# Gates of the merge made ahead of the pooling, top-k rounds tile by tile: a reordering of filler work in a fused three-branch decoder layer

## The chip, the cores and the metric

The kernel runs on one core of one Trainium2 chip. A core has five engines that run their own queues in order: TensorE (PE, matmuls, with its weight loads shown as PEld), VectorE (DVE), ScalarE (ACT), GpSimd (POOL) and SyncE (SP), which issues DMA transfers; POOL issues some as well. The time is the device time of one execution in microseconds, and the median of several executions counts. Less is better.

## The reference

One decoder layer on x of 512 x 1024 float32. One input projection makes all that three branches need; each branch is gated, projected, weighted by a per-channel sigmoid and added; an output projection, a scaled residual and a LayerNorm end it.

```
u = x @ w_in + b_in                       # split into 19 pieces
y_a = pool_mixer(a_x) * silu(a_z)         # A: trailing means over windows 2, 4, 8, 16 (4 groups of 128 channels),
                                          #    minus x, then a 128x128 matmul per group
y_b = dsa(b_q, b_k, b_v, i_q, i_k, i_w) * silu(b_z)
                                          # B: an indexer scores all keys, each query keeps its 128 best causal
                                          #    keys, 8 heads attend to these with one shared key and value
y_c = nsa(c_q, ..., c_g) * silu(c_z)      # C: 8 heads in 2 groups: compressed blocks, selected blocks, window;
                                          #    three softmaxes, gated per head
g = sigmoid(g_merge)                      # 512 x 3 x 1024
m = g[:,0] * (y_a @ w_pa) + g[:,1] * (y_b @ w_pb) + g[:,2] * (y_c @ w_pc)
out = layernorm(2**0.25 * x + m @ w_o)
```

Top-k is min(256, 512 // 4) = 128 keys, so the first tile of 128 queries needs no selection: top-k concerns the query tiles j = 1, 2 and 3, whose score rows are 256, 384 and 512 long.

## The kernel before

Everything large is kept transposed, channels on partitions, the 512 positions along the free axis. float32 matmuls are made from two-part splits: a high part and a remainder, three matmuls for one product (`mm3`, lines 68 to 70). x is split once into xh and xl. The weights come in tiles of 128 output channels x 1024 inputs; `load_w` (line 87) loads one into a staging tile, ACT copies the high part (line 93), POOL subtracts for the remainder (line 95; DVE does it at the start and end of the kernel). There are 2 staging tiles and 3 each of high and low parts, so the next tiles are made while one is used.

`dense(i)` (line 142) is one such tile: 8 steps, each of three 128x128 by 512 matmuls into one PSUM bank (pool `pd`, 3 banks), with a `yield` after each step. On it stand: `queries` (ACT and DVE split the result), `silu2` (two ACT passes into two tiles, one DVE pass), `gate_d` (line 597: one ACT tanh of a merge gate into a tile `tg` of tag "b"), `pool_x` (line 556), `pool_z` (line 577), `keypair`. `pool_x(g)` copies the result to SBUF on ACT, makes the trailing sums by g + 1 shifted adds with small copies on POOL (lines 566, 567), the mean minus x by four DVE instructions (lines 570 to 573) and splits it into `ph` (ACT line 64, DVE line 65). `pool_y(g)` (line 582) is one step: three matmuls of `ph` with the group's matrix, then DVE at line 588 multiplies with the gate `za` of `pool_z(g)`, and a split.

`merge(br, d)` (line 621) is one of 8 channel tiles of one branch's projection: before its own 4 steps (`branch_d`: a weight tile of 128 x 512, tile `pp` in PSUM, one DVE pass at line 614) it runs `merge_g(br, d + 1)`, the 8 steps of the next tile's gate, so a merge has 12 steps. For branches 2 and 1, POOL adds the product to the sum (line 632).

Attention is made in units (`Unit`, line 410): kind "c" for branch C, two groups g, query tiles j = 3, 2, 1, 0, two parts br (selected blocks together with the compressed ones, and window); then kind "b" for branch B, g = 0 and 1, j = 0 to 3. A unit has one or two sub-units. `front(u)` makes scores on PE into a PSUM bank (pool `pq`, 4 banks; line 441), adds the mask and takes the maximum on DVE (line 443), exponentiates on ACT (line 448), normalises into high and low float16 parts `pc` or `pb` (ACT line 460, DVE line 462) and transposes them by a DMA on SP's queue. `back` is the product with the values on PE (line 479), two sub-units later (`LAG = 2`), with `finish` (line 534) behind it.

**Order.** PE's order is the program's own (`manual_schedule`), the other engines' is made by a planner that simulates the program; `tc.high_priority()` lifts the weight splits and evacuations there. The dense work between the attention is a list of generators, the stream `F` (line 731). The loop over units gives it credit: `F.step(3.25)` after each half of a front, `F.step(2)` after a sub-unit, 0.3 per step of a back; in the index stage 2 per score. One credit is one `yield`. A string in the list, "c0" or "c1", is a mark: as long as the flag of that name is not set, the stream stops there and its credit is dropped (line 694). The flag c0 (c1) is set when the last unit of group 0 (1) of branch C is finished. `F.until` runs the stream on to a named item where a unit needs it.

Top-k takes 16 rounds per tile, each of one MAX8 and one MATCH_REPLACE8 (with the load of its values) over the score row `acc{j}` in place; `topk_end` turns the marked row into the mask of unit b{g}{j}. The list `rounds` (line 742) goes through j = 1, 2, 3 in turn. `tk(2.3)` after each sub-unit, ordered behind its last DVE instruction, takes 2.3 rounds on average; whatever is left goes at the first unit b of j > 0 (`tk(100)`).

Of the kernel before, what the change touches and what calls it, by code (L numbers as in the profile page):

```python
# [7 lines left out]
F32 = mybir.dt.float32  # L8
# [11 lines left out]
KT = D // 128  # L20
# [14 lines left out]
def trunk(ctx, tc, a, out, dbg=None):  # L35
# [12 lines left out]
    def big(tag, name, dt=F32, shape=(128, 2, 512)):  # L48
        return bp.tile(list(shape), dt, tag=tag, name=name, bufs=BUFS[tag])
# [13 lines left out]
    def split(h, l, src):  # L63
        nc.scalar.activation(h, src, AF.Copy)
        nc.vector.tensor_sub(l, src, f(h))  # L65
# [76 lines left out]
    def dense(i, s0=0, ps=None):  # L142
        wh, wl = early[i][1:] if i in early else load_w(a["wt"][i], 1024, f"w{i}")
        ps = (ps or dps)(f"d{i}")
        n = S - s0
        for k in range(KT):
            w = slice(k * 128, k * 128 + 128)
            mm3(ps[:, :n], wh[:, w], wl[:, w], X(0, k, s0), X(1, k, s0), k == 0, k == KT - 1)
            yield
        return ps[:, :n], bias[:, i:i + 1]  # L150
# [388 lines left out]
    def psum_acc():  # L539

        turn[0] ^= 1
        return ACC[:, turn[0]]
# [51 lines left out]

    M32 = []

    def gate_d(d, br):
        i = I_G + 3 * d + br
        ps, b = yield from dense(i)
        t = big("b", "tg", F32, (128, 512))  # L600
        with tc.high_priority():
            nc.scalar.activation(t, ps, AF.Tanh, scale=0.5, bias=bhalf[:, i:i + 1])
        return t

    def branch_d(d, br, Y, t, dst):
        wh, wl = load_w(a["wp"][br, d], 512, f"wp{br}")
        ps = dps("pp")
        for e in range(4):
            w = slice(e * 128, e * 128 + 128)
            yh, yl = Y[e // 2]  # L610
            mm3(ps, wh[:, w], wl[:, w], yh[:, e % 2], yl[:, e % 2], e == 0, e == 3)
            yield
        with tc.high_priority():
            nc.vector.scalar_tensor_tensor(dst, t, 1.0, ps, op0=OP.add, op1=OP.mult)  # L614

    tg, YS, MH, ML = {}, {}, [], []

    def merge_g(br, d):
        tg[br, d] = yield from gate_d(d, br)

    def merge(br, d):
        if d + 1 < KT:
            yield from merge_g(br, d + 1)
        t = tg[br, d]
        if br == 0:
            if d % 2 == 0:
                M32.append(big("t", f"m{d}"))
            yield from branch_d(d, 0, YA, t, M32[d // 2][:, d % 2])
        else:
            yield from branch_d(d, br, YS[br], t, t)  # L630
            m = M32[d // 2][:, d % 2]
            nc.gpsimd.tensor_add(m, m, t)  # L632
            if br == 1:
                if d == 0:
                    MH.extend(big("pt", f"mh{i}", F32R, (128, 4, 512)) for i in range(2))
                    ML.extend(big(t, f"ml{i}", F32R) for i, t in enumerate("sspp"))
                split(MH[d // 4][:, d % 4], ML[d // 2][:, d % 2], m)
                dbg(f"m{d}", m)
# [84 lines left out]
    for n in (2, 1, 1, 1, 1, 1, 2):  # L723
        for _ in range(n):
            st.step()
        for _ in range(n):
# [2 lines left out]
    mcmp, rowv = small["mcmp"].rearrange("p (j n) -> p j n", j=NT), small["rowv"]  # L729
    POOL[0] = True  # L730
    F = Stream([(compress_in, I_KC, "k"), (vscales,), (compress_in, I_VC, "v"), (f_zc, 0, 0), (compress_mid, "k"),
                (f_zc, 0, 1), (compress_k,), (compress_mid, "v"), (f_qc, 1, 0), (f_qc, 1, 1), (f_pool,), (compress_v,),
                (pool_x, 0), (pool_x, 1), (pool_z, 0), (pool_z, 1), (f_kk, 1), (pool_y, 0), (f_zc, 1, 0), (pool_y, 1),
                (pool_x, 2), (pool_x, 3), (f_zc, 1, 1), (pool_z, 3), (pool_z, 2), (pool_y, 2), (f_qb, 0, 0), (pool_y, 3),
                (merge_g, 0, 0), "c0", (f_qb, 0, 1)] + [(merge, 0, d) for d in range(4)] +
               [(f_zb, 0, 0), (f_zb, 0, 1)] + [(merge, 0, d) for d in range(4, 7)] +
               [(merge_g, 2, 0), (merge, 0, 7), "c1", (f_qb, 1, 0), (f_qb, 1, 1), (f_zb, 1, 0), (f_zb, 1, 1)] +
               [(merge, 2, d) for d in range(KT)])
    ix = Stream([(index_scores, j) for j in (1, 2, 3)])
    while ix.step():  # L740
        F.step(2)
    rounds = [(topk_round, j) for _ in range(16) for j in (1, 2, 3)] + [(topk_end, j) for j in (1, 2, 3)]
    tkn = [0.0]

    def tk(n):
        tkn[0] += n
        while rounds and tkn[0] >= 1:
            tkn[0] -= 1
            fn, j = rounds.pop(0)
            fn(j)  # L750

    work = []
    for g in range(2):
# [11 lines left out]
    def flush(limit):  # L765

        while backs and backs[0][0] <= limit:
            _, un, w = backs.pop(0)
            if limit == 1000:
                F.step(8)  # L770
            kind, g, j, br = w
            if kind == "c":
                F.until(("vscales",), ("compress_v",), ("f_zc", g, 0), ("f_zc", g, 1))
            for _ in un.back(br == 0):
                F.step(0.3)
            if kind == "b":
                F.until(("f_zb", g, 0), ("f_zb", g, 1))
                finish(un.acc, j, zb[g], YB[g])
            elif br == 1:
                cmps[g, j].back(un.acc)  # L780
                finish(un.acc, j, zc[g], YC[g])
                if j == 0:
                    flags.add(f"c{g}")
                    if g == 1:
                        split_y(2, YC)

    for w in work:
        kind, g, j, br = w
        if kind == "c":
            if br == 0:  # L790
                accs[w[:3]] = psum_acc()
            F.until(("compress_k",), *([("f_kk", g)] if g else []), *([("f_qc", g, e) for e in range(2)] if g else []))
            if j == 3 and br == 0:
                YC.append(big("t", f"yc{g}"))
            gv = GS[:, j, :].rearrange("p (h b) -> p h b", b=3)
            if br == 0:
                cmps[g, j] = Compressed(g)
            un = Unit(f"c{g}{j}{br}", accs[w[:3]], j, qc[g], kk[g][br], cmask[:, (3 - j) * 128:],
                      1 + 2 * br + g, gv[:, 4 * g:4 * g + 4, 1 + br], None if br else cmps[g, j])
        else:  # L800
            F.until(("f_qb", g, 0), ("f_qb", g, 1))
            if j == 0:
                YB.append(big("t", f"yb{g}"))
            if j:
                tk(100)
            un = Unit(f"b{g}{j}", psum_acc(), j, qb[g], KB[0], cmask[:, 384:] if j == 0 else negm[j],
                      0, None)
        for u in range(un.nsub):
            for _ in un.front(u):
                F.step(3.25)  # L810
            with tc.issue_after(un.last.ins):
                tk(2.3)
            nsub += 1
            F.step(2)
            flush(nsub - LAG)
        backs.append((nsub, un, w))
# [165 lines left out]
```

## Time and profile before

| | |
|---|---|
| median of 3 runs | 550.96 us (550.22 to 551.14) |
| profiled execution | 547.52 us, span 545.7 us |
| PE busy, mean granted clock | 519.2 us (95%), 0.976 |
| DVE, ACT, POOL busy | 381.6 (70%), 278.7 (51%), 217.8 us (40%) |
| dense matmuls (tile d) of weight tiles, lines 68 to 70 | 3 x 424, 0.39 us each |
| weight splits on POOL, 128x1024 / 128x512 | 41 x 2.44 us / 16 x 1.28 us |

The profile is of one execution. A row of a list in order of time begins with the start and the duration in us; a line in square brackets is the wait in front and what ended it. A matmul's duration overlaps the next one's: the distance of two starts is what it costs. "x8" counts instructions. Rows by group give busy us and the mean in ns.

### The profile page before, as it was taken

What the parts mean: (1) busy time and instruction counts of PE and PEld (TensorE: products, weight loads), DVE (VectorE), ACT (ScalarE), POOL (GpSimd) and SP (SyncE); (2) the same over time, 40 slices, a digit from 0 to 9 for tenths busy, and PEclk for the clock granted to TensorE, in tenths of its full rate; (3) what the DMA queues carried; (4) which work ended last, traced back from release to release, by engine and by line L of the source; (5) the groups of instructions that cost most, each with busy time, mean ns of one, the idle gap of its engine ahead of it and who ended that gap; (6) DMA issues with size and microseconds to landing.
All of it is one profiled execution on the core that took longest, in us unless ns stands there. A gap on an engine that the chain in (4) does not pass through costs nothing.

```text
span 545.7 us, 7778 instructions
## 1 busy us (share of the span) xinstructions
PE 519.2 (95%) x2718; PEld 420.2 (77%) x2718; DVE 381.6 (70%) x928; ACT 278.7 (51%) x561; POOL 217.8 (40%) x190
## 2 busy tenths in 40 slices
PE   7999989989999876999999999999999999999993
PEld 4899878868778654877778877787878888887883
DVE  5774898999999999888766466666441544545366
ACT  6783466655565475546566585765632333442000
POOL 0325433465557441134544355355564211316043
PEclk8999999989999997899999999999999999999997
DMA  7622331436545243365544445545553336454012
GB/s 271 261 77 78 115 117 59 121 79 154 95 114 126 64 116 82 84 165 129 154 102 114 123 130 132 126 117 127 139 140 96 117 111 207 164 185 144 1 60 94
DMA packets 82135, 66.72 MB, mean 122 GB/s; under 512 B 67184, under 2 KB 68656, under 8 KB 82096
## 3 DMA queue, kind: packets, MB, share of 16 engines
q1 hardware_dynamic: 74912, 40.54, 27.8%
q0 software_dynamic: 7184, 25.69, 15.4%
q8 instruction: 21, 0.34, 0.3%
q14 instruction: 18, 0.15, 0.1%
HBM read 47.87 MB, written 2.10 MB: 92 GB/s over the span
## 4 chain that ended last, share of the span: by engine, by line
PE 56%; DVE 9%; DMA 2%; ACT 1%; issue 1%; DVEq 0%; ACTq 0%
PE d L68 10%; PE d L70 10%; PE d L69 10%; PE pp L68 4%; PE pp L70 4%; PE pp L69 4%; PE acc L479 3%; PE wo L70 2%; PE wo L68 2%; PE wo L69 2%; PE qkb L441 2%; PE qkc L441 2%; DMA wo_st<-in_wo_dram 1%; DVE acc L306 1%; DVE m L305 1%
## 5 line engine op out<-in xcount | busy, mean ns | idle before, releaser
L68 PE MATMUL d<-xh,w_h 128*128 128x512 f32 (+1 forms) x424 | 168.6, 398 | 5.6 <-DVE za L588 2.8
L70 PE MATMUL d<-xh,w_l 128*128 128x512 f32 (+1 forms) x424 | 166.2, 392 | 0.0
L69 PE MATMUL d<-xl,w_h 128*128 128x512 f32 (+1 forms) x424 | 166.0, 392 | 0.0
L95 POOL TENSOR_TENSOR w_l<-w_st,w_h 128x1024 fp32r<-128x1024 f32 x41 | 99.8, 2436 | 130.1 <-ACT w_h L93 129.2
L68 PEld LDWEIGHTS d<-xh,w_h 128*128 128x128 f32 x424 | 80.5, 190 | 23.7 <-DVE za L588 3.3
L70 PEld LDWEIGHTS d<-xh,w_l 128*128 128x128 f32 x424 | 80.4, 190 | 17.5 <-DVE w_l L95 0.4
L69 PEld LDWEIGHTS d<-xl,w_h 128*128 128x128 f32 x424 | 80.5, 190 | 14.0
L93 ACT ACTIVATE w_h<-w_st 128x1024 fp32r<-128x1024 f32 x53 | 56.1, 1059 | 52.0 <-DMA w_st<-in_wt_dram 23.4
L448 ACT ACTIVATE qkc<-qkc,nb 128x512 f32<-128x512 f32 (+3 forms) x64 | 32.1, 502 | 44.3 <-DVE nb L443 28.6
L632 POOL TENSOR_TENSOR m<-m,tg 128x512 f32<-128x512 f32 x16 | 21.7, 1355 | 56.2 <-DVE tg L614 54.5
L95 POOL TENSOR_TENSOR wp_l<-wp_st,wp_h 128x512 fp32r<-128x512 f32 x16 | 20.5, 1281 | 53.9 <-ACT wp_h L93 53.9
L462 DVE SCALAR_TENSOR_TENSOR pc<-qkc,r,pc 128x512 f16<-128x512 f32 (+3 forms) x64 | 32.6, 543 | 8.6 <-ACT pc L460 8.3
L460 ACT ACTIVATE pc<-qkc,r 128x512 f16<-128x512 f32 (+3 forms) x64 | 29.6, 525 | 12.7 <-issue 5.5
L443 DVE CUSTOM_DVE_ANT_0 qkc<-qkc,cmask 128x512 f32<-128x512 f32 (+3 forms) x64 | 31.3, 490 | 4.4 <-PE qkc L441 4.0
L95 DVE TENSOR_TENSOR w_l<-w_st,w_h 128x1024 fp32r<-128x1024 f32 x12 | 15.6, 1306 | 19.4 <-ACT w_h L93 19.4
L448 ACT ACTIVATE qkb<-qkb,nb 128x128 f32<-128x128 f32 (+3 forms) x32 | 16.0, 500 | 23.3 <-DVE nb L443 23.0
L92 POOL DMA_DIRECT2D w_st<-in_wt_dram x41 | 23.3, 568 | 10.2 <-POOL w_l L95 6.8
L70 PE MATMUL wo<-woh,ml 128*128 128x512 f32 (+1 forms) x72 | 26.4, 367 | 0.3 <-DVE ml L65 0.3
L69 PE MATMUL wo<-wol,mh 128*128 128x512 f32 (+1 forms) x72 | 26.3, 366 | 0.0
L68 PE MATMUL wo<-woh,mh 128*128 128x512 f32 (+1 forms) x72 | 26.3, 365 | 0.0
L306 DVE MATCH_REPLACE8 acc<-m,acc 128x256 f32<-128x256 f32 (+2 forms) x48 | 25.7, 540 | 0.0
L479 PEld LDWEIGHTS <-vh 128*64 128x64 f16 x240 | 13.8, 110 | 15.1 <-issue 15.1
(245 smaller groups left out, 1031.7 us busy)
## 6 DMA issues: line engine op xcount, KB each, us to landing
w_st<-in_wt_dram POOLq DMA_DIRECT2D x41, 512.0 KB, 3.7
w_st<-in_wt_dram SPq DMA_DIRECT2D x12, 512.0 KB, 4.6
wp_st<-in_wp_dram POOLq DMA_DIRECT2D x16, 256.0 KB, 3.0
wo_st<-in_wo_dram SPq DMA_DIRECT2D x8, 512.0 KB, 3.5
xst<-in_xT_dram SPq DMA_DIRECT2D x8, 256.0 KB, 5.1
wp_st<-in_wp_dram SPq DMA_DIRECT2D x8, 256.0 KB, 2.6
z<-in_x_dram SPq DMA_DIRECT2D x4, 512.0 KB, 4.9
wvst<-in_wve_dram SPq DMA_DIRECT2D x4, 320.0 KB, 6.9
```

Of the source, the lines that this page charges most:

```text
L68: nc.tensor.matmul(ps, wh, rh, start=start, stop=False)
L69: nc.tensor.matmul(ps, wh, rl, start=False, stop=False)
L70: nc.tensor.matmul(ps, wl, rh, start=False, stop=stop)
L92: (nc.gpsimd if POOL[0] else nc.sync).dma_start(st, src)
L93: nc.scalar.activation(h[:, :n], st, AF.Copy)
L95: eng.tensor_sub(l[:, :n], st, f(h[:, :n]))
L306: nc.vector.match_replace(negm[j], m8, negm[j], MARK)
L443: nc.vector.tensor_tensor_reduce(sc[i], sc[i], self.mask, -0.125, 3e38, OP.add, OP.min, nb[:, i:i + 1])
L448: nc.scalar.activation(sc[i], sc[i], AF.Exp, scale=-1.0, bias=nb[:, i:i + 1], accum_out=den[:, i:i + 1])
L460: nc.scalar.activation(p[:, 0, i], sc[i], AF.Copy, scale=r[:, i:i + 1])
L462: self.last = nc.vector.scalar_tensor_tensor(p[:, 1, i], sc[i], r[:, i:i + 1], p[:, 0, i], op0=OP.mult, op1=OP.subtract)
L479: nc.tensor.matmul(self.acc[64 * i:64 * i + 64], v[:, k, self.vs * 64:self.vs * 64 + 64], pw[:, z, i, k], start=first, stop=False, skip_gr ...
```

## The change

The order of the filler stream and the rate of the top-k rounds are changed; no instruction is added or dropped.

- A new item `early_g(br, d)` makes the gate of channel tile d into one half of a tile of tag "s" (two tiles hold four gates). The four gates d = 0 to 3 of branch 0 stand between the compression and the pooling's items, those of branch 2 just in front of the mark "c1". `merge` skips the gate of the next tile where it is there already: merge(0, 0 to 2) and merge(2, 0 to 2) have 4 steps instead of 12.
- The pooling's items come later and in another order: pool_z and pool_y follow their pool_x more closely, and `f_pool` (the load and split of the pooling matrices) later as well. f_kk(1) and f_zc(1, 0) come ahead of them, f_qb(0, 0) goes behind "c0".
- Top-k: all rounds of j = 1 and 2 in turn with their ends, then those of j = 3. After each sub-unit 1.7 rounds instead of 2.3, and at unit b{g}{j} only what is left of tile j (`tk_until`).

```diff
--- before.py
+++ after.py
@@ -594,10 +594,10 @@
 
     M32 = []
 
-    def gate_d(d, br):
+    def gate_d(d, br, t=None):
         i = I_G + 3 * d + br
         ps, b = yield from dense(i)
-        t = big("b", "tg", F32, (128, 512))
+        t = big("b", "tg", F32, (128, 512)) if t is None else t
         with tc.high_priority():
             nc.scalar.activation(t, ps, AF.Tanh, scale=0.5, bias=bhalf[:, i:i + 1])
         return t
@@ -618,8 +618,16 @@
     def merge_g(br, d):
         tg[br, d] = yield from gate_d(d, br)
 
+    EG = {}
+
+    def early_g(br, d):
+
+        if d % 2 == 0:
+            EG[br] = big("s", f"eg{br}{d}", F32)
+        tg[br, d] = yield from gate_d(d, br, EG[br][:, d % 2])
+
     def merge(br, d):
-        if d + 1 < KT:
+        if d + 1 < KT and (br, d + 1) not in tg:
             yield from merge_g(br, d + 1)
         t = tg[br, d]
         if br == 0:
@@ -729,17 +737,19 @@
     mcmp, rowv = small["mcmp"].rearrange("p (j n) -> p j n", j=NT), small["rowv"]
     POOL[0] = True
     F = Stream([(compress_in, I_KC, "k"), (vscales,), (compress_in, I_VC, "v"), (f_zc, 0, 0), (compress_mid, "k"),
-                (f_zc, 0, 1), (compress_k,), (compress_mid, "v"), (f_qc, 1, 0), (f_qc, 1, 1), (f_pool,), (compress_v,),
-                (pool_x, 0), (pool_x, 1), (pool_z, 0), (pool_z, 1), (f_kk, 1), (pool_y, 0), (f_zc, 1, 0), (pool_y, 1),
-                (pool_x, 2), (pool_x, 3), (f_zc, 1, 1), (pool_z, 3), (pool_z, 2), (pool_y, 2), (f_qb, 0, 0), (pool_y, 3),
-                (merge_g, 0, 0), "c0", (f_qb, 0, 1)] + [(merge, 0, d) for d in range(4)] +
-               [(f_zb, 0, 0), (f_zb, 0, 1)] + [(merge, 0, d) for d in range(4, 7)] +
-               [(merge_g, 2, 0), (merge, 0, 7), "c1", (f_qb, 1, 0), (f_qb, 1, 1), (f_zb, 1, 0), (f_zb, 1, 1)] +
-               [(merge, 2, d) for d in range(KT)])
+                (f_zc, 0, 1), (compress_k,), (compress_mid, "v"), (f_qc, 1, 0), (f_qc, 1, 1), (compress_v,),
+                (early_g, 0, 0), (f_kk, 1), (early_g, 0, 1), (f_pool,), (f_zc, 1, 0), (pool_x, 0), (early_g, 0, 2),
+                (pool_z, 0), (pool_x, 1), (early_g, 0, 3), (pool_y, 0), (pool_z, 1), (f_zc, 1, 1), (pool_x, 2), (pool_y, 1),
+                (pool_z, 2), (pool_x, 3), (pool_y, 2), (pool_z, 3), (pool_y, 3),
+                "c0", (f_qb, 0, 0), (f_qb, 0, 1)] + [(merge, 0, d) for d in range(3)] + [(f_zb, 0, 0), (f_zb, 0, 1)] +
+               [(merge, 0, d) for d in range(3, 7)] + [(early_g, 2, 0), (merge, 0, 7)] +
+               [(early_g, 2, d) for d in range(1, 4)] +
+               ["c1", (f_qb, 1, 0), (f_qb, 1, 1), (f_zb, 1, 0), (f_zb, 1, 1)] + [(merge, 2, d) for d in range(KT)])
     ix = Stream([(index_scores, j) for j in (1, 2, 3)])
     while ix.step():
         F.step(2)
-    rounds = [(topk_round, j) for _ in range(16) for j in (1, 2, 3)] + [(topk_end, j) for j in (1, 2, 3)]
+    rounds = [(topk_round, j) for _ in range(16) for j in (1, 2)] + [(topk_end, 1), (topk_end, 2)]
+    rounds += [(topk_round, 3)] * 16 + [(topk_end, 3)]
     tkn = [0.0]
 
     def tk(n):
@@ -748,6 +758,11 @@
             tkn[0] -= 1
             fn, j = rounds.pop(0)
             fn(j)
+
+    def tk_until(j):
+        while (topk_end, j) in rounds:
+            fn, i = rounds.pop(0)
+            fn(i)
 
     work = []
     for g in range(2):
@@ -802,14 +817,14 @@
             if j == 0:
                 YB.append(big("t", f"yb{g}"))
             if j:
-                tk(100)
+                tk_until(j)
             un = Unit(f"b{g}{j}", psum_acc(), j, qb[g], KB[0], cmask[:, 384:] if j == 0 else negm[j],
                       0, None)
         for u in range(un.nsub):
             for _ in un.front(u):
                 F.step(3.25)
             with tc.issue_after(un.last.ins):
-                tk(2.3)
+                tk(1.7)
             nsub += 1
             F.step(2)
             flush(nsub - LAG)
```

## The prediction

> **What bounds the kernel now.** I read the busy table first, then the table by stage, then TensorE's (PE's) order of time where a stage is not full.
>
> ```profile
> span 545.7 us, 7778 instructions
> PE 519.2 (95%) x2718; PEld 420.2 (77%) x2718; DVE 381.6 (70%) x928; ACT 278.7 (51%) x561; POOL 217.8 (40%) x190
> ...
> 100.00:125.00 25.00, 22.54 (x102) 17.77 (x103) 24.86 (x58) 14.13 (x28) 13.13 (x12) 0.93 0.49 116
> 175.00:200.00 25.00, 19.71 (x96) 15.05 (x94) 24.52 (x74) 12.80 (x37) 11.98 (x12) 0.93 0.32 88
> 200.00:225.00 25.00, 19.15 (x101) 14.28 (x102) 23.01 (x69) 13.85 (x38) 4.79 (x4) 0.80 0.33 80
> 225.00:520.00 295.00, 294.73 (x1510) 236.99 (x1510) 169.06 (x417) 145.50 (x295) 115.53 (x89) 1.00 0.46 128
> ```
>
> The columns of a stage are its length, then busy time of PE, weight load, DVE, ACT and POOL, the granted clock, DMA. From 225 to 520 us PE has no hole (294.73 of 295). Its holes lie in 100 to 225, where DVE is 92 to 99% busy: there DVE sets the pace, everywhere behind it PE does. So only two things count: how much hole between 100 and 225 closes, and whether a new hole opens.
>
> ```profile
> 115.46 0.73 PE L441 MATMUL qkc<-kw,cq 128*128 128x512 f32 x2 [2.46 <-DVE pc L462]
> ...
> 187.28 0.50 PE L68 MATMUL d<-xh,w_h 128*128 128x512 f32 x1 [2.55 <-ACT z L153]
> ...
> 195.82 0.39 PE L69 MATMUL d<-xl,w_h 128*128 128x512 f32 x1
> 196.04 0.39 PE L70 MATMUL d<-xh,w_l 128*128 128x512 f32 x1
> ...
> 200.40 0.50 PE L68 MATMUL d<-xh,w_h 128*128 128x512 f32 x1 [2.82 <-DVE za L588]
> ...
> 209.15 0.39 PE L70 MATMUL d<-xh,w_l 128*128 128x512 f32 x1
> ...
> 213.43 2.31 PE L441 MATMUL qkc<-ks,cq 128*128 128x512 f32 x4 [2.70 <-DVE pc L462]
> 217.98 0.43 PE L479 MATMUL acc<-ptc,vh 128*64 128x256 f16 x2 [2.23 <-DMA ptc<-pc]
> 220.77 0.63 PE L68 MATMUL d<-xh,w_h 128*128 128x512 f32 x1
> ```
>
> The brackets give the wait in front and what ended it. Hole A waits for pc, which frees the score buffer. Holes B (on z) and C (on za) wait for PSUM buffers that are freed late because DVE is late: za is DVE's own, and ACT, in order, held z behind score work that wanted DVE's nb. Hole D, two waits, is another kind: from 209.4 to 220.8 no dense matmul (tile d) runs at all. The filler stream F stands at its mark "c0" there. Counting its yields against the credit given in the loop over units (3.25 twice and 2 per sub-unit, 0.3 per back step, 48 in the index stage): before "c0" lie 167 steps, the flag is set when 181 could have been done, so about 14 are lost.
>
> The stages around A, B and D, for their holes in full and for the clock, which falls behind them:
>
> ```profile
> 112.90:120.00 7.10, 4.63 (x14) 3.56 (x14) 7.07 (x21) 3.03 (x7) 2.10 (x4) 0.78 0.73 144
> 184.60:195.00 10.40, 7.53 (x36) 5.47 (x36) 10.02 (x35) 8.83 (x23) 4.54 (x4) 0.84 0.16 53
> 210.00:222.50 12.50, 7.35 (x33) 4.96 (x34) 10.62 (x39) 7.83 (x20) 1.82 (x2) 0.60 0.22 50
> ```
>
> Holes: 7.10 - 4.63 = 2.47, 10.40 - 7.53 = 2.87, 12.50 - 7.35 = 5.15, and C's 2.82. Busy time times what the clock lacks: 4.63 x 0.22 = 1.0 at A, 7.53 x 0.16 = 1.2 at B, 7.35 x 0.40 = 2.9 at D. So A is worth 3.5, B and C 6.9, D 8.05: 18.45 us is the most that this stage can give.
>
> **The change part by part.**
>
> *Filler moved ahead (D).* The four gates of branch 0 (32 steps) now stand before "c0"; f_qb(0,0) (8) goes behind it, and merge_g(0,0) was there already: 167 + 24 - 8 = 183 steps, 2 more than the 181 wanted. D closes: +8.05. One step is three matmuls at 0.23 us apart (195.82 to 196.04 above), 0.68 us; the total of PE's work is unchanged. A gate tile costs what it did: its load and split on POOL, its split on ACT and one tanh travel with it, only to another tile (tag "s", free after the values). The load of pool_w on SP's queue comes 25 steps later, behind a few transposes, and its first user, pool_y(0), 48 steps after it. f_qb(0,0) is needed by unit b00, some 80 steps later. The four gates of branch 2 come ahead of "c1", where the replayed count loses no step before or after: 0; what is left for the end shrinks from 25 steps to 10, and 10 + 16 gate steps (18 us) still hide the split of YB.
>
> *Top-k (A, B, C).* A round is one MAX8 and one MATCH_REPLACE8:
>
> ```profile
> L305 DVE MAX8 m<-acc 128x8 f32<-128x512 f32 x16 | 10.8, 676 | 0.0
> L306 DVE MATCH_REPLACE8 acc<-m,acc 128x512 f32<-128x512 f32 x16 | 10.8, 672 | 0.0
> L305 DVE MAX8 m<-acc 128x8 f32<-128x384 f32 x16 | 8.7, 544 | 0.0
> L306 DVE MATCH_REPLACE8 acc<-m,acc 128x384 f32<-128x384 f32 x16 | 8.7, 541 | 0.0
> L305 DVE MAX8 m<-acc 128x8 f32<-128x256 f32 x16 | 6.6, 411 | 0.0
> L306 DVE MATCH_REPLACE8 acc<-m,acc 128x256 f32<-128x256 f32 x16 | 6.5, 406 | 0.0
> ```
>
> 1.35, 1.09 and 0.82 us for j = 3, 2, 1. Over the 13 sub-units of group c0: before 2.3 x 13 = 29 rounds, 10 x 0.82 + 10 x 1.09 + 9 x 1.35 = 31.2 us; after 1.7 x 13 = 22 rounds of j = 1 and 2, 21.0 us: 10.2 us less DVE work. The pooling is also later: at F's step 150 (about B) pool_x 2 and 3 have yet to come (3.7 us each of DVE by the three long rows of pool_x(3) below), pool_z 2 and 3 and a pool_y (four passes of the 0.69 of L65 below): 10 us more. The holes in front of D are 8.2 us; 20 us less on DVE by then closes B and C: +6.9 (bounds: half of it, and all). For A only the first sub-unit's second round (1.09) and the split of pool_w (about 0.7, the size of the L65 row below) go from in front of pc: 1.8 of the 2.46, and with it the slow clock: +2.8 (bounds 0 and 3.5).
>
> *Where these rounds go.* They now run through sub-unit 29 instead of 22: 1.7 x 1.35 = 2.3 us more per sub-unit in 23 to 29, where DVE and PE stand so:
>
> ```profile
> 275.80:284.60 8.80, 8.80 (x61) 6.71 (x60) 5.55 (x24) 5.47 (x14) 1.93 (x3) 1.00 0.55 144
> 284.60:291.10 6.50, 6.50 (x35) 5.51 (x35) 4.04 (x12) 3.95 (x12) 2.86 (x2) 1.00 0.31 95
> 291.10:300.00 8.90, 8.90 (x55) 7.22 (x53) 7.09 (x30) 5.95 (x19) 4.79 (x4) 1.00 0.45 109
> 324.00:331.00 7.00, 7.00 (x37) 5.52 (x35) 6.30 (x10) 4.28 (x8) 5.93 (x3) 1.00 0.57 150
> ```
>
> The last is a stretch of b02. 5.55 + 2.3 of 8.8, 4.04 + 2.3 of 6.5, then 9.4 of 8.9 and 8.6 of 7.0: over by 0.5 and 1.6, and the lag of two sub-units (some 16 us) between a front and its back carries that. Cost 0; without the lag, 2.1.
>
> *The new tight place.* PE's order is the program's, so a matmul whose input is late holds all behind it. pool_x(3) used to end at step 125 and pool_y(3) to stand at 159. Now they are 10 steps apart (173 and 183), with only pool_y(2), the 8 steps of pool_z(3), two fronts and a back between: 9 x 0.68 + 2 x 0.45 + 1.1 = 8.1 us. The chain it must cover, from the old run:
>
> ```profile
> 167.03 0.68 ACT L153 ACTIVATE x<-d,bias 128x512 f32<-128x512 f32 x1
> ...
> 168.94 1.05 POOL L566 TENSOR_TENSOR xs<-x 128x511 f32<-128x511 f32 x1
> ...
> 174.08 2.54 POOL L95 TENSOR_TENSOR w_l<-w_st,w_h 128x1024 fp32r<-128x1024 f32 x1 [2.26 <-ACT w_h L93]
> ...
> 179.53 0.19 POOL L567 COPY xs<-xs 128x8 f32<-128x8 f32 x1
> ...
> 185.50 0.69 DVE L572 SCALAR_TENSOR_TENSOR x<-xs,x 128x512 f32<-128x512 f32 x1
> 186.22 2.33 DVE L573 COPY x<-pe 128x15 f32<-128x15 f32 x1
> ...
> 189.90 0.69 DVE L65 TENSOR_TENSOR ph<-x,ph 128x512 fp32r<-128x512 f32 x1
> ```
>
> 23.6 us from 167.03 to 190.6. On POOL 12.7, of which 4.8 (2.26 + 2.54) are a weight split put in the middle: 7.9 without. On DVE and ACT 10.9 as it ran; bare, about 2.5 (an estimate: 0.7 + 0.7 for L572 and L65, 0.7 for the split on ACT, as long as L153, 0.4 for the copy and the small ones). Where DVE's steps land is the planner's choice, which I cannot see. So pool_y(3) waits between 7.9 + 2.5 - 8.1 = 2.3 (1 if POOL does not first finish a split) and 23.6 - 8.1 = 15.5. I take POOL without the split and the DVE part halfway, 7.9 + 6.7 - 8.1 = 6.5, and the clock's loss at B, 1.2: -7.7. pool_y(2) has 17 steps and four fronts, 16 us, against 15.4 that the x(2) chain took: 0, at most 2.
>
> ```profile
> 118.89 2.38 POOL L95 TENSOR_TENSOR w_l<-w_st,w_h 128x1024 fp32r<-128x1024 f32 x1 [5.00 <-ACT w_h L93]
> ...
> 118.95 2.87 DVE L572 SCALAR_TENSOR_TENSOR x<-xs,x 128x512 f32<-128x512 f32 x1
> ```
>
> The same L572 takes 0.69 alone and 2.87 beside a split on POOL. Such a hold, 2.2 us, lies inside the 10.9, and half of it inside my middle. The Trainium skill, GPSIMD Engine Reference, section 8 Key points, says that GpSimd shares its SBUF interfaces with VectorE's two-input instructions; the trace agrees (2.87 against 0.69). If by it both long DVE steps were held in full, the wait would be 7.9 + 2.5 + 4.4 - 8.1 = 6.7, next to what I take. The skill's TensorE: Matmul & The Clock Gate, section Why this matters for your kernels, asks for no idle gap above about 3 us; the trace differs, 2.46 and 2.55 were followed by lost clock and 2.82 was not, so that a hole left at A could still cost clock, which the page would give as nothing.
>
> *Three merges in a row.* merge(0,0..2), and later merge(2,0..2), now have 4 steps each (about 4 us with a sub-unit's attention in it) and want one 256 KB load, ACT split, POOL split and evacuation in that time.
>
> ```profile
> L95 POOL TENSOR_TENSOR wp_l<-wp_st,wp_h 128x512 fp32r<-128x512 f32 x16 | 20.5, 1281 | 53.9 <-ACT wp_h L93 53.9
> ...
> wp_st<-in_wp_dram POOLq DMA_DIRECT2D x16, 256.0 KB, 3.0
> ```
>
> 3.0 + 1.3 + the ACT split (0.7 at most, as L153) is 5.0 us per tile and, with two staging buffers, 2.5; with a wait in each engine's order 3.5: it fits barely. I take -1 (bounds 0 and -3).
>
> **Sum.** 8.05 + 2.8 + 6.9 - 7.7 - 1 = 9.05 us less. The profiled execution took 547.5 (span 545.7 and 1.8 around it), 3.4 below the median of the runs, 550.96. The same difference off the median: 541.9, say 542.
>
> **The rivals.** (1) pool_x(3) is handled at once, the wait is about 1 and costs no clock: 17.75 - 1 - 1 = 15.75 less, 535. For it: DVE has 20 us less to do; against: two sub-units of 512 keys fall into just that place. (2) A weight split is put between the four adds again, as at 174.08: 12.7 + 6.7 - 8.1 = 11.3 and 1.2: 17.75 - 12.5 - 1 = 4.25 less, 546.5; with DVE as slow as it was, 15.5 + 1.2, nothing is left, 551. For it: that is the order of the old run. (3) The other side: sub-units 23 to 29 come to be paced by DVE, because a round in front of the masks delays the scores more than the lag allows. 7 x 2.3 = 16 on the path, 9 gained: 7 slower, 558. It decides from 9 of the 16 on. Against: DVE is 62 to 90% busy in the rows above, and with 2.3 rounds each in 225 to 268 PE had no hole. (4) It does not do what it says: the stream still runs dry at "c0", as the margin is 2 steps: 8.05 less gain, 550.
>
> **Chances.** Forecast (538 to 545) 0.46, (1) 0.24, (2) at 546.5 0.15, (2) at 551 and (4) 0.08, (3) 0.07. A difference under 0.2% (1.1 us) cannot be told from none here. Faster 0.85, same 0.08, slower 0.07. The range reaches from a little below (1) to the slow end of (2): 533.5 to 550.5.
>
> **What would show it.** Right: dense matmuls without a break from 205 to 220 us; PE's waits on z L153, on za L588 and on the transpose gone; DVE under 95% in 100 to 200; a wait of pool matmuls on ph (L65) some 6 us long around 205 to 215, the longest left; top-k until some 325 us and still no hole behind 225. Wrong: no wait on ph (then 535), or PE waiting for pc or qkb scores behind 260 (then (3)).

## The result, and the profile after

The changed kernel takes 540.38 us, the median of 4 runs (540.3 to 541.13), against 550.59 (550.12 to 551.14) for the kernel before: ratio 0.9817, 95% interval 0.98 to 0.9834. In a second comparison, beside later experiments, it took 541.39 (539.09 to 542.44) against 547.92 (545.2 to 549.68): ratio 0.9894 (0.9849 to 0.9939). The gain is thus 10.2 us in the one comparison and 6.5 in the other; the forecast was 9 less, 542.0, in a range of 533.5 to 550.5. In two of the runs further down one execution was far slower than the others (1309 us in e2, 854 us in the first run of e4) and is left out of the figures.

The page of the changed kernel and its table by stage (length, then busy time of PE, weight load, DVE, ACT and POOL, clock, DMA share, GB/s):

```profile
span 538.5 us, 7778 instructions
PE 517.8 (96%) x2718; PEld 419.3 (78%) x2718; DVE 377.3 (70%) x928; ACT 278.1 (52%) x561; POOL 215.9 (40%) x190
...
100.00:125.00 25.00, 25.00 (x131) 20.36 (x130) 24.09 (x65) 17.29 (x32) 11.11 (x9) 1.00 0.62 140
...
175.00:200.00 25.00, 25.00 (x147) 20.58 (x146) 20.75 (x81) 17.56 (x51) 14.75 (x14) 1.00 0.39 110
200.00:225.00 25.00, 17.88 (x78) 12.73 (x77) 20.04 (x53) 12.67 (x27) 12.04 (x16) 0.80 0.31 77
...
225.00:520.00 295.00, 293.01 (x1499) 234.75 (x1499) 187.25 (x447) 141.02 (x289) 110.98 (x87) 1.00 0.47 125
```

The first two stages are full now, DVE has air behind 125 us (20.75 of 25 in 175 to 200, before 24.52), and nearly all that is left of the holes behind 100 us stands in 200 to 225; 225 to 520 has 2.0 us, of which 1.5 are one wait at 302 us. Behind 225, DVE does 18 us more than before (187.25 against 169.06): the top-k rounds that were put later.

PE's waits by what ended them (total, times, longest), first the kernel before:

```profile
PE qkc L441 <- DVE pc L462: 5.5, 3, 2.7
PE d L68 <- DVE za L588: 2.8, 1, 2.8
PE d L68 <- ACT z L153: 2.6, 1, 2.6
PE acc L479 <- DMA ptc<-pc: 2.2, 1, 2.2
```

The same view of the changed kernel:

```profile
PE pool L68 <- ACT ph L64: 6.9, 2, 6.5
PE pp L68 <- ACT tg L602: 1.5, 1, 1.5
```

The four of before are holes A to D with a small one on pc (0.3, between B and C), 13.1 us, and none of them is left. In their place stand one wait of the pool matmuls on ph, and a small one on a gate's tanh, tg.

The changed kernel around that wait, in order of time on POOL, ACT and PE (start, duration; in brackets the wait in front):

```profile
206.11 2.44 POOL L95 TENSOR_TENSOR w_l<-w_st,w_h 128x1024 fp32r<-128x1024 f32 x1 [2.58 <-ACT w_h L93]
...
213.12 1.27 POOL L95 TENSOR_TENSOR wp_l<-wp_st,wp_h 128x512 fp32r<-128x512 f32 x1 [0.47 <-ACT wp_h L93]
...
215.53 0.66 POOL L567 COPY xs<-xs 128x8 f32<-128x8 f32 x1
...
205.92 0.68 ACT L153 ACTIVATE x<-d,bias 128x512 f32<-128x512 f32 x1
...
218.43 0.63 ACT L64 ACTIVATE ph<-x 128x512 fp32r<-128x512 f32 x1 [3.21 <-DVE x L573]
...
219.11 0.80 PE L68 MATMUL pool<-ph,plhl 128*128 128x512 f32 x1 [6.50 <-ACT ph L64]
```

From the evacuation of pool_x(3) at 205.92 to the high part of ph at 218.43 + 0.63 = 219.06 pass 13.1 us. POOL is through at 215.53 + 0.66 = 216.19, 10.3 after the start: it first had to finish a split (206.11 + 2.44 = 208.55), and another fell between the third and the fourth add (213.12). DVE and ACT took 2.9 of it. PE stood from 219.11 - 6.50 = 212.6, so it had covered 6.7.

The clock behind that wait, in slices of 5 us:

```profile
215.00:220.00 5.00, 0.89 (x2) 0.45 (x2) 4.12 (x7) 1.37 (x4) 2.39 (x4) 0.52 0.26 59
220.00:225.00 5.00, 5.00 (x12) 3.94 (x13) 2.67 (x6) 1.41 (x3) 0.00 (x0) 0.50 0.00 0
225.00:230.00 5.00, 5.00 (x22) 4.05 (x22) 3.42 (x10) 1.87 (x4) 0.00 (x0) 0.95 0.33 74
```

Lost: 0.89 x 0.48 + 5.00 x 0.50 + 5.00 x 0.05 = 3.2 us. With the 6.5 itself the wait costs 9.7, on paper. In the second profile of the same kernel the same wait of 6.50 lost 2.2 us of clock (2.78 x 0.50 + 5.00 x 0.17).

### The profile page after: what moved, and what is told of

Same layout as the page of the kernel before. It is cut to its first block, busy times and chain, and to the rows that moved or that the text cites. A ratio compares the mean times of both kernels' runs of the same rounds, so it can differ in the third digit from the quotient of the medians.

```text
span 538.5 us, 7778 instructions
## 1 busy us (share of the span) xinstructions
PE 517.8 (96%) x2718; PEld 419.3 (78%) x2718; DVE 377.3 (70%) x928; ACT 278.1 (52%) x561; POOL 215.9 (40%) x190
## 4 chain that ended last, share of the span: by engine, by line
PE 87%; DVE 5%; DMA 3%; ACT 2%; issue 1%; POOL 1%; SPq 0%; DVEq 0%; ACTq 0%; POOLq 0%
PE d L68 18%; PE d L69 17%; PE d L70 17%; PE acc L479 4%; PE pp L68 4%; PE qkc L441 4%; PE pp L69 4%; PE pp L70 4%; PE wo L70 3%; PE wo L69 2%; PE wo L68 2%; PE qkb L441 2%; DMA wo_st<-in_wo_dram 2%; DMA xst<-in_xT_dram 1%; PE acc L529 1%; PE ve L69 1%
## 5 line engine op out<-in xcount | busy, mean ns | idle before, releaser
L95 POOL TENSOR_TENSOR w_l<-w_st,w_h 128x1024 fp32r<-128x1024 f32 x41 | 98.1, 2394 | 128.9 <-ACT w_h L93 124.8
L640 POOL TENSOR_TENSOR m<-m,tg 128x512 f32<-128x512 f32 x12 | 16.5, 1378 | 53.7 <-DVE tg L614 53.6
L92 POOL DMA_DIRECT2D w_st<-in_wt_dram x41 | 23.3, 569 | 10.2 <-POOL w_l L95 5.9
L305 DVE MAX8 m<-acc 128x8 f32<-128x256 f32 (+2 forms) x48 | 25.4, 549 | 0.0
L68 PE MATMUL pp<-yh,wp_h 128*128 128x512 f32 x64 | 25.3, 395 | 0.0
L69 PE MATMUL pp<-yl,wp_h 128*128 128x512 f32 x64 | 25.0, 390 | 0.0
```

The costliest lines, as they stand in the source:

```text
L68: nc.tensor.matmul(ps, wh, rh, start=start, stop=False)
L69: nc.tensor.matmul(ps, wh, rl, start=False, stop=False)
L95: eng.tensor_sub(l[:, :n], st, f(h[:, :n]))
L305: nc.vector.max(m8, negm[j])
```

## The experiments

The theory is the sum of the prediction: the filler moved ahead closes D, the lighter DVE closes A to C, and the wait on ph gives a part back, which could be had again. A first rival is that one of the two parts alone does it all. A second came up with the first results: the wait on ph is a symptom of work that is late anyway, so that to take it away brings much less than it lasts. For the last four runs the two sides have letters, P (the wait is on the path and costs what it lasts) and Q (DVE's work around the pooling sets the pace).

| run | before, same chip | this, median (lowest to highest) | ratio (95%) |
|---|---|---|---|
| e1, top-k alone | 549.68 | 538.4 (535.1 to 541.0) | 0.9798 (0.9739 to 0.9857) |
| e2, filler order alone | 549.68 | 539.64 (539.1 to 540.2) | 0.982 (0.9767 to 0.9874) |
| e3, gates ahead, old pooling, old top-k | 549.68 | 537.23 (536.6 to 539.4) | 0.979 (0.9732 to 0.9847) |
| e4, pool_y(3) later | 549.68 | 537.75 (537.4 to 537.9) | 0.9787 (0.9735 to 0.984) |
| e4 again | 548.46 | 536.8 (535.8 to 538.5) | 0.978 (0.9717 to 0.9843) |
| e5, without the rounds of j = 3 | 548.46 | 537.09 (535.8 to 538.3) | 0.9781 (0.972 to 0.9843) |
| e6, e3 with the new top-k | 548.46 | 536.78 (536.1 to 539.3) | 0.9785 (0.9721 to 0.9849) |
| e8, two gates at c0 alone | 548.46 | 544.02 (540.9 to 545.1) | 0.9892 (0.9813 to 0.9971) |
| the changed kernel again | 547.92 | 541.39 (539.1 to 542.4) | 0.9894 (0.9849 to 0.9939) |
| e9, pool_z(3) ahead of pool_x(3) | 547.92 | 540.77 (540.6 to 541.3) | 0.9878 (0.9841 to 0.9915) |
| e10, pool_x(2), (3) earlier | 547.92 | 538.16 (536.4 to 539.0) | 0.9824 (0.9782 to 0.9867) |
| e11, e10 with pool_y(3) later | 547.92 | 537.89 (537.2 to 539.5) | 0.9828 (0.9787 to 0.9868) |

**e1: the top-k's part alone**, in the kernel before.

```diff
-    rounds = [(topk_round, j) for _ in range(16) for j in (1, 2, 3)] + [(topk_end, j) for j in (1, 2, 3)]
+    rounds = [(topk_round, j) for _ in range(16) for j in (1, 2)] + [(topk_end, 1), (topk_end, 2)]
+    rounds += [(topk_round, 3)] * 16 + [(topk_end, 3)]
...
-                tk(100)
+                tk_until(j)
...
-                tk(2.3)
+                tk(1.7)
```

> Only the top-k part of the change: rounds by tile, 1.7 per sub-unit, the old order of the filler. Theory (two separate gains, DVE relief and filler): the stop of the dense work at c0 (hole D, 5.15 us and 2.9 of clock) stays, hole A shrinks, B and C lose a half or more with 10 us less DVE work: 544 to 547. Rival (the order of the filler does everything): 550, holes as before. Rival (top-k moved late costs at the end): over 551, with holes behind 260.

Measured 538.4, less than expected, and by the ratio as much as the whole change. PE's waits in e1:

```profile
PE qkc L441 <- DVE pc L462: 4.2, 2, 2.7
PE acc L479 <- DMA ptc<-pc: 1.7, 1, 1.7
...
PE d L68 <- DVE za L588: 1.2, 1, 1.2
...
PE d L68 <- ACT z L153: 0.6, 1, 0.6
```

A is gone, B shrinks from 2.6 to 0.6 and C from 2.8 to 1.2, while the small wait on pc between them grows from 0.3 to 1.5: of the 8.2 us of A to C with that wait, 3.3 are left. The stream still stands dry at "c0" (the two waits of D, 1.7 and 2.7 at 205 to 209 us, and no dense step between them), so D is not mended here; it is smaller by 0.5 us.

**e2: the filler's order alone**, the changed kernel with the old top-k.

```diff
-    rounds = [(topk_round, j) for _ in range(16) for j in (1, 2)] + [(topk_end, 1), (topk_end, 2)]
-    rounds += [(topk_round, 3)] * 16 + [(topk_end, 3)]
+    rounds = [(topk_round, j) for _ in range(16) for j in (1, 2, 3)] + [(topk_end, j) for j in (1, 2, 3)]
...
-                tk_until(j)
+                tk(100)
...
-                tk(1.7)
+                tk(2.3)
```

> Only the filler's new order, the old top-k (2.3 rounds per sub-unit, j = 1, 2, 3 in turn). Theory: D closes (8 less), but DVE has 10 us more to do in group c0 than in the changed kernel, so the wait of pool_y(3) on ph grows from 6.5 to 8 or 10 and A stays: 543 to 547. Rival (the order does everything): 540.4 as the whole change.

Measured 539.64. PE's longest wait in e2,

```profile
PE pool L68 <- ACT ph L64: 8.8, 2, 7.3
```

and the stage from 175 us:

```profile
175.00:200.00 25.00, 25.00 (x147) 20.54 (x145) 23.07 (x85) 16.50 (x50) 14.03 (x15) 1.00 0.43 108
```

With 2.3 rounds per sub-unit A, B and C are closed too, although DVE does 23.07 of 25: it is enough that the pooling comes later. So the two parts don't add up. Each takes all or most of the overload from DVE that made A to C, and the second finds little left to close. What the filler's order closes besides, D, it gives back in the wait on ph and the clock behind it, which e1 does not have. The wait on ph is longer with the old top-k (7.3 for 6.5).

**e3: gates ahead, the pooling's items in the order of before**, old top-k (its lines as in e2, not shown again).

```diff
-                (early_g, 0, 0), (f_kk, 1), (early_g, 0, 1), (f_pool,), (f_zc, 1, 0), (pool_x, 0), (early_g, 0, 2),
-                (pool_z, 0), (pool_x, 1), (early_g, 0, 3), (pool_y, 0), (pool_z, 1), (f_zc, 1, 1), (pool_x, 2), (pool_y, 1),
-                (pool_z, 2), (pool_x, 3), (pool_y, 2), (pool_z, 3), (pool_y, 3),
+                (early_g, 0, 0), (early_g, 0, 1), (early_g, 0, 2), (early_g, 0, 3), (f_pool,),
+                (pool_x, 0), (pool_x, 1), (pool_z, 0), (pool_z, 1), (f_kk, 1), (pool_y, 0), (f_zc, 1, 0), (pool_y, 1),
+                (pool_x, 2), (pool_x, 3), (f_zc, 1, 1), (pool_z, 3), (pool_z, 2), (pool_y, 2), (pool_y, 3),
```

> The gates ahead, but behind them the pooling in its old order, pool_x(3) ended 26 steps before pool_y(3), and the old top-k. Theory: D closes and there is no long wait on ph, but DVE is as full as before, so waits like B and C come back somewhere in the pooling: 541 to 545. Rival (the running dry at c0 was no cost of its own, DVE would have set the pace there anyway): 548 to 551.

Measured 537.23, less than expected. Here 25 steps lie between pool_x(3) and pool_y(3), 9 in the changed kernel, and still pool_y(3), at 216.54, waits for ph:

```profile
PE pool L68 <- ACT ph L64: 4.5, 1, 4.5
PE qkc L441 <- DVE pc L462: 1.6, 1, 1.6
```

ACT copies the result of pool_x(3) at 191.76 and POOL is through at 205.64, but DVE comes to L572 only at 211.10 and to L573 at 215.10, with top-k rounds of all three tiles and score work in between. Here it is DVE's queue that makes ph late. The 1.6 on pc is what is left of A.

**e6: e3 with the new top-k.** The edit is that of e3 above, with the changed kernel's rounds and rate kept.

> Gates ahead, the pooling behind them in its old order, and the new top-k: the best of both parts if they add. Theory (both parts cure one and the same overload of DVE, so they don't add, but with 10 us less top-k the wait of the pool matmuls on ph, 4.5 us, should shrink): 533 to 536. Rival (nothing to be gained on top): 537 to 538.

Measured 536.78, between the two expectations. Its waits:

```profile
PE pool L68 <- ACT ph L64: 2.1, 1, 2.1
PE pp L68 <- ACT tg L602: 1.5, 1, 1.5
```

The lighter DVE now takes the wait from 4.5 to 2.1, and A is closed, yet the ratio moves only from 0.979 to 0.9785. By medians from different chips it is some 4 us below the changed kernel.

**e8: D alone.** The kernel before, with two more gates in front of "c0" and nothing else moved (`early_g` as in the change, not shown).

```diff
-                (merge_g, 0, 0), "c0", (f_qb, 0, 1)] + [(merge, 0, d) for d in range(4)] +
+                (early_g, 0, 0), (early_g, 0, 1), (early_g, 0, 2), "c0", (f_qb, 0, 1)] + [(merge, 0, d) for d in range(4)] +
```

> The kernel before with two more gates of branch 0 just in front of the mark c0 (183 steps instead of 167) and nothing else: pooling and top-k as before. It isolates the running dry. Theory (D is worth its holes and clock, 8 us, and only D closes): 541 to 544, A, B and C as before. Rival (DVE sets the pace of that stage in any case): 547 to 550.

Measured 544.02: 4.4 less than before (by the interval 1.6 to 10.3). PE's waits:

```profile
PE d L68 <- DVE za L588: 2.9, 1, 2.9
PE qkc L441 <- DVE pc L462: 2.8, 2, 2.5
PE qkb L441 <- DVE pb L462: 2.7, 1, 2.7
PE d L68 <- ACT z L153: 2.5, 1, 2.5
```

D is closed, as the count of steps said, and A, B and C stand at their old lengths. A wait of 2.7 on pb, at 323 us, where the kernel before had no hole, and one of 0.9 on kw at 151 us are new and take part of the gain; why they come stays open.

**e4: pool_y(3) behind f_qb(0, 0)**, run on two chips.

```diff
-                (pool_z, 2), (pool_x, 3), (pool_y, 2), (pool_z, 3), (pool_y, 3),
-                "c0", (f_qb, 0, 0), (f_qb, 0, 1)] + ...
+                (pool_z, 2), (pool_x, 3), (pool_y, 2), (pool_z, 3),
+                "c0", (f_qb, 0, 0), (pool_y, 3), (f_qb, 0, 1)] + ...
```

> The whole change, with pool_y(3) moved by 8 steps, behind f_qb(0,0), just past the mark c0. Theory (the wait of pool_y(3) on ph, 6.5 us, and the clock lost behind it, some 3 us, are all that is left of the stage): both vanish, 530 to 533. Rival (DVE is late there anyway, the wait moves to the next matmul that needs a DVE or ACT result): 537 to 540, with a new wait of several us between 205 and 235.

> The same kernel as the run before it (pool_y(3) behind f_qb(0,0)), for its profile and more times. It took 537.6 where 530 to 533 were expected. Theory (a wait is left that was not on the list: another PE hole in 190 to 240, or holes of the late sub-units): the profile shows holes and lost clock of some 8 us together. Rival (matmuls that run closer together are slower, no hole left): no hole over 1 us, but a lower clock or longer matmuls.

Measured 537.75 and 536.8: faster than the changed kernel, but by 3 or 4 us and not by 8 to 9. The second run's waits:

```profile
PE pool L69 <- DVE ph L65: 2.2, 2, 1.9
...
PE pool L68 <- ACT ph L64: 1.4, 2, 1.0
```

Of the 6.5 more than half went, but pool_y(3), 8 steps later, still waits 1.0 for the high and 1.9 for the low part of ph. With the 1.5 on tg and 2.7 us of clock lost between 220 and 230 (2.92 x 0.36 + 5.00 x 0.32) the profile has some 8 us of holes and lost clock behind 200 us, as the theory of the second run said; its rival, no hole over 1 us, is excluded.

**e5: the changed kernel without the 16 rounds of j = 3**, so the selection of query tile 3 is left out.

```diff
-    rounds += [(topk_round, 3)] * 16 + [(topk_end, 3)]
+    rounds += [(topk_end, 3)]
```

> The changed kernel without the 16 rounds of tile j = 3 (query tile 3 of branch B then attends to all its keys: that part of the selection is left out), 21.6 us of DVE work taken from sub-units 20 to 29. Theory (these rounds cost next to nothing there): 537 to 540.4, at most the wait of pp on tg (1.5 us, near 302) gone. Rival (the late sub-units are paced by DVE): 530 or less.

Measured 537.09. The wait of the merge on tg is gone; that on ph stays, 6.9 in all. In the changed kernel it stood here:

```profile
302.14 0.53 PE L68 MATMUL pp<-yah,wp_h 128*128 128x512 f32 x1 [1.47 <-ACT tg L602]
```

That is what the late rounds cost on PE's path: 1.5 us, not nothing. They need the new stream beside them: e1 has the late rounds in the old stream, e2 and e3 the new stream with the early rounds, and none of the three has this wait. The rest of the difference, some 2 us by medians from different chips, has no wait of its own in the profile.

**The changed kernel again, and e9: pool_z(3) ahead of pool_x(3).** This takes 8 steps of cover from in front of pool_y(3) and is to price the wait.

```diff
-                (pool_z, 2), (pool_x, 3), (pool_y, 2), (pool_z, 3), (pool_y, 3),
+                (pool_z, 2), (pool_z, 3), (pool_x, 3), (pool_y, 2), (pool_y, 3),
```

> The changed kernel as it is, once more, so that the three variants beside it are compared with it on one chip. Both theories: 540.4 again (539 to 541), the wait of a pool matmul on ph 6.5 us.

> The changed kernel with pool_z(3) put ahead of pool_x(3) instead of behind it: 8 steps less between pool_x(3) and pool_y(3), the same work. Theory P (the wait is on the path and costs what it lasts): the wait grows by 8 x 0.68 = 5.4 to some 12 us and the time by the same, to 546. Theory Q (around the pooling DVE's work sets the pace, and the wait only shows its backlog; shifting matmuls from behind it to in front of it moves little): the wait grows, but holes behind it go, time 540 to 542.

The changed kernel took 541.39 and e9 540.77: 5.4 us of cover less made no difference to the time. The wait itself grew by 2.3 us, from 6.5 to 8.76, and not by the 5.4 that P priced, so the run refutes P's forecast of the wait, but is a weak test of what a wait costs. e9 in order of time on ACT, POOL and PE:

```profile
210.87 0.68 ACT L153 ACTIVATE x<-d,bias 128x512 f32<-128x512 f32 x1
...
219.30 0.63 ACT L64 ACTIVATE ph<-x 128x512 fp32r<-128x512 f32 x1 [4.40 <-DVE x L573]
...
211.07 1.26 POOL L95 TENSOR_TENSOR wp_l<-wp_st,wp_h 128x512 fp32r<-128x512 f32 x1 [0.92 <-ACT wp_h L93]
...
219.99 0.79 PE L68 MATMUL pool<-ph,plhl 128*128 128x512 f32 x1 [8.76 <-ACT ph L64]
```

The chain from evacuation to ph takes 219.93 - 210.87 = 9.1 us here, 13.1 in the changed kernel: pool_x(3) begins 5 us later and ends 0.9 later. The split of wp_l (211.07) is done ahead of the adds, and DVE, which stood idle for the last 3.2 us of them, has nothing else in hand when they end. So the chain's length depends on what POOL and DVE still have in hand, and the wait is no fixed price for a distance in steps.

**e10: pool_x(2) and pool_x(3) 16 steps earlier; e11: the same with pool_y(3) behind f_qb(0, 0).**

```diff
-                (pool_z, 0), (pool_x, 1), (early_g, 0, 3), (pool_y, 0), (pool_z, 1), (f_zc, 1, 1), (pool_x, 2), (pool_y, 1),
-                (pool_z, 2), (pool_x, 3), (pool_y, 2), (pool_z, 3), (pool_y, 3),
+                (pool_z, 0), (pool_x, 1), (early_g, 0, 3), (pool_y, 0), (pool_z, 1), (pool_x, 2), (pool_x, 3), (f_zc, 1, 1), (pool_y, 1),
+                (pool_z, 2), (pool_y, 2), (pool_z, 3), (pool_y, 3),
```

> The changed kernel with pool_x(2) and pool_x(3) 16 steps earlier, ahead of f_zc(1,1), so that 26 steps instead of 10 stand between pool_x(3) and pool_y(3). Theory P: the wait of 6.5 us falls under 1 and takes its lost clock (some 3 us) with it: 531 to 533. Theory Q: the wait goes, but PE waits elsewhere between 185 and 225 us (for pc, z or za) for DVE, which then has the same work in the same time: 537 to 539.

> The one before with pool_y(3) also behind f_qb(0,0), 8 steps later. Theory P: nothing is left to win over it, 531 to 533. Theory Q: DVE's backlog has 8 more steps to be worked off, 1 to 3 us less than the one before.

Measured 538.16 and 537.89, where theory P said 531 to 533 and Q 537 to 539. The wait on ph is gone in both. In e10 PE, POOL and DVE do this instead:

```profile
192.62 1.04 PE L500 MATMUL sc<-ks,cq 128*128 128x32 f32 x8
...
201.10 0.79 PE L68 MATMUL d<-xh,w_h 128*128 128x512 f32 x1 [5.51 <-DVE cs L501]
...
190.83 2.37 POOL L95 TENSOR_TENSOR w_l<-w_st,w_h 128x1024 fp32r<-128x1024 f32 x1 [2.73 <-ACT w_h L93]
...
194.85 1.05 POOL L566 TENSOR_TENSOR xs<-xs 128x510 f32<-128x510 f32 x1
...
191.81 1.41 DVE L570 TENSOR_TENSOR pe<-xs,small 128x7 f32<-128x7 f32 x1
...
194.97 0.96 DVE L573 COPY x<-pe 128x7 f32<-128x7 f32 x1
...
196.63 1.08 DVE L65 TENSOR_TENSOR ph<-x,ph 128x512 fp32r<-128x512 f32 x1 [0.63 <-ACT ph L64]
...
200.77 0.28 DVE L501 TENSOR_TENSOR cs<-sc,small 128x128 f32<-128x128 f32 x1
```

The compressed scores lie finished in a PSUM bank of the dense pool from 193.7 us on. The one DVE instruction that frees the bank comes at 200.77, behind the steps of pool_x(2), of which L570 and L573 last long beside POOL's work, behind its split, which waits for ACT, and behind two top-k rounds and the score work of the unit. PE waits 5.5 us for the bank. A wait on ph has become a wait for a PSUM bank that DVE frees late, 1.0 us shorter; 3.2 us of time is the gain. e11, with more distance still, has the same wait on the bank (5.4) and brings nothing over e10. So Q's forecast holds here, though the wait that it saw coming (on pc, z or za) is one on cs.

## Why the prediction was right, and where its steps were off

**What bounds the kernel** was right: behind 100 us PE's holes lie before 225 only, made by DVE's lateness and by the stream running dry. A to D are all closed, 18.45 us as listed; the prediction had counted 17.75. Two of its signs came out otherwise: DVE is under 95% from 125 to 200 us (79 to 83%), but not in 100 to 125 (24.09 of 25), where PE is full all the same; and the last top-k round stands at 344 us, not at 325.

**D.** The count of steps holds (no dense gap at "c0", and e8 closes D with nothing but two more gates there). Its price of 8.05 is neither confirmed nor refuted: e8 gains 4.4 (1.6 to 10.3), with 2.7 and 0.9 spent on new waits.

**A, B, C** were put down to top-k and pooling together, 20 us less of DVE's work. e2 shows that the later pooling is enough, and e1 that the lighter top-k is nearly so (3.3 of 8.2 us left). The terms of the sum were right for the whole change, but would have been wrong for each half: with half the change, 544 to 547 (e1) and 543 to 547 (e2) were expected, and 538.4 and 539.64 came out.

**The wait on ph** was forecast as 7.9 + 6.7 - 8.1 = 6.5 and measured as 6.50, but by terms that made up for one another: POOL took 10.3 instead of 7.9 (a split in front and one between the adds, rival (2)'s mechanism in a mild form), DVE and ACT 2.9 instead of 6.7, and the cover was 6.7 instead of 8.1. The place and the kind of the wait were foreseen; that its length agrees to the tenth is luck. The clock behind it was mis-sized: 3.2 us (2.2 in the second profile) instead of 1.2, because a wait of 6.5 was priced by the loss behind one of 2.5. pool_y(2) waited 0.39 + 0.23, inside the 0 to 2 given.

**Three merges in a row, -1:** the wait of 1.5 is on a gate's tanh at 302 us and goes with the rounds of j = 3 (e5), so it is not the merges' loads but a small piece of **rival (3)**, the late rounds, which was priced at 16 us on the path. In order of time the tanh stands on ACT behind score work that had waited for DVE. The table of that stage has DVE at

```profile
300.00:325.00 25.00, 23.53 (x134) 18.44 (x133) 21.92 (x63) 13.09 (x39) 10.78 (x8) 1.00 0.48 137
```

21.92 of 25, so the cost of 0 for the late rounds was wrong by 1.5.

**Sum.** By the two profiled executions the span fell from 545.7 to 538.5, 7.2 us: 18.45 of holes and clock closed, and opened 6.5 + 3.2 for the wait, 0.6 for pool_y(2) and 1.5 for the merge, 11.8, which leaves 6.7 (5.0, if the 1.7 us of clock lost at 75 us, shown at the end, are taken as part of it). Slices of 5 us put the clock that the kernel before lost behind A, B and D at 6.2 instead of the 5.1 counted, which makes it 7.8 (6.1); what makes up the difference to 7.2 isn't resolved. The terms that opened came to 11.8, where 8.7 (7.7 and 1) had been forecast. The forecast of 9.05 lies between the 6.5 and the 10.2 of the two comparisons of medians. Rivals (1) and (4) are excluded by the wait and by the closed D.

**What the change gave away.** The reading that "wait plus clock", 9.7 us, can be had back was wrong: e4, e10 and e11 take the wait away or most of it, and win 3 to 4. By the profiles the waits on pool matmuls or the bank and the clock lost behind them, in 195 to 230 us, are 10.3 us in the changed kernel (9.3 in its second profile), 6.2 in e4 and 8.0 in e10. These differences are near to what was won, so that a wait may well cost what it lasts; the step that failed is that the edit would leave none in its place. e9 doesn't fit as well: it loses 11.7 there, and its time is no longer. e10's rows show where the lateness goes, e9's that a chain behind which less is queued is shorter. e10 beside the changed kernel on one chip is 538.16 (536.4 to 539.0) against 541.39 (539.1 to 542.4). So e10 beats both kernels; e11 and, by medians from other chips, e1, e3, e4 and e6 do so as well, and which of them is best can't be told. The top-k's part alone, e1, would have done as much as the whole change.

**Open.** Why the second comparison shows 6.5 and the first 10.2: the changed kernel differs by 1.0 us between the two, and the kernel before by 2.7. Some of the spread arises ahead of all that the change moves: the matmul `ve<-wvh,xh` starts at 46.18 us in the one profile of the changed kernel and at 45.39 in the other, and between 44.4 and 47.6 in the kernel before and in ten of the runs above.

## What to carry to other kernels

When two edits relieve the same engine in the same stretch, price them together: either may close most or all of the holes, and the sum of the two halves is not the whole. A wait on an engine's late result is no prize of its length: ask what that engine does next and who waits for that, since the lateness moves on to another buffer (here from ph to a PSUM bank). Price the clock behind a wait by waits of its own length, and as a range, and look for the few microseconds of a weight split that the order of another engine can slide into a chain.

## What was unexpected of the hardware

The loss of clock behind a short wait is not the same from one execution to the next. The same wait of 1.2 us on bkl stands at 72 us in both profiles of the changed kernel. In the first, in order of time:

```profile
72.76 0.25 PE L69 MATMUL cpk<-bkl,w1h 128*64 128x62 f32 x1 [1.21 <-DVE bkl L65]
```

and the slice behind it:

```profile
75.00:80.00 5.00, 5.00 (x28) 4.36 (x27) 4.95 (x8) 3.97 (x7) 1.04 (x2) 0.66 0.31 106
```

The same kernel run again, in order of time:

```profile
71.99 0.25 PE L69 MATMUL cpk<-bkl,w1h 128*64 128x62 f32 x1 [1.23 <-DVE bkl L65]
```

and the slice behind it:

```profile
75.00:80.00 5.00, 4.75 (x26) 3.92 (x25) 4.97 (x8) 3.54 (x7) 0.57 (x1) 1.00 0.29 105
```

In the one 5.00 x 0.34 = 1.7 us are lost, in the other none. Hole A of before (2.46) had a clock of 0.78 in the stretch behind it; the stage of e8 that holds the same hole of 2.5 ran at 1.00:

```profile
100.00:125.00 25.00, 22.53 (x108) 17.99 (x108) 24.76 (x60) 13.64 (x27) 12.84 (x13) 1.00 0.46 109
```

So the prediction's remark that 2.46 and 2.55 cost clock and 2.82 did not marks no threshold. The Trainium skill, TensorE: Matmul & The Clock Gate, section Why this matters for your kernels, asks for no idle gaps over about 3 us; by these rows shorter ones can be followed by a loss too, and need not be.

DVE's short steps of the pooling last several times longer beside POOL's work. In e10 L570 took 1.41 and L573 0.96 us; in e9, with POOL done:

```profile
217.88 0.17 DVE L570 TENSOR_TENSOR pe<-xs,small 128x15 f32<-128x15 f32 x1 [3.19 <-POOL xs L567]
...
219.10 0.17 DVE L573 COPY x<-pe 128x15 f32<-128x15 f32 x1
```

Both long ones end with the POOL instruction that had begun before them: L570 at 191.81 + 1.41 = 193.22, POOL's split at 190.83 + 2.37 = 193.20; L573 at 194.97 + 0.96 = 195.93, POOL's add at 194.85 + 1.05 = 195.90. So does the L573 of 2.33 us in the kernel before, at 188.55, beside this split, which ends at 188.53:

```profile
186.15 2.38 POOL L95 TENSOR_TENSOR w_l<-w_st,w_h 128x1024 fp32r<-128x1024 f32 x1 [6.42 <-ACT w_h L93]
```

L573 has a single input, so that by these rows such holds aren't confined to instructions with two.
